# A two-layer hybrid decoder trunk on one core: every read of SBUF by GpSimd in the mixing stages goes to ScalarE and VectorE

## The chip, the core and the metric

The kernel runs on one core of a Trainium2 chip. The core's engines each work through their own instruction queue in order and meet at semaphores: TensorE (PE in the profile, with its weight loads as PEld), VectorE (DVE), ScalarE (ACT), GpSimd (POOL) and SyncE (SP), which issues the DMAs. The metric is the device time of one execution in microseconds. The kernel before takes 1375.88 us (median of three runs, 1375.21 to 1383.43).

## What is computed

Two decoder layers over 512 tokens of width 1024, in float32. The reference, cut:

```python
for l in range(DEPTH):                                   # DEPTH = 2
    h = rmsnorm(x, g_mix[l])
    (cq, ckv, kr, aq, ak, av, qi, ki, wi, rq, rk, rv, rg) = split(h @ w_in[l])
    # A) latent attention, 8 heads: low-rank q (768) and kv (256), rotary part of 32
    q  = rmsnorm(cq, g_q[l]) @ w_uq[l];  kv = rmsnorm(ckv, g_kv[l]) @ w_ukv[l]
    o_a = mla_attention(q_nope, rope(q_rope), k_nope, rope(kr), v)
    # B) sparse attention, 4 heads: an indexer scores all keys, the best 128 of a query are kept
    score = einsum(wi, relu(rope(qi) . rope(ki)));  sel = top_k(score, 128)
    o_b = dsa_attention(rope(aq), rope(ak), av, sel)
    # C) retention, 4 heads, with group norm and swish gate
    o_c = silu(rg) * groupnorm(retention(rope(rq), rope(rk), rv))
    x = x + concat(o_a, o_b, o_c) @ w_out[l]
    hf = rmsnorm(x, g_mlp[l])
    x = x + square(relu(hf @ w_ff1[l])) @ w_ff2[l]
return rmsnorm(x, g_final)
```

## The kernel before, in words

Activations are held transposed: a tile has 128 features on the partitions and the 512 tokens in its columns. To keep float32 precision, each operand of a matmul is split into a high half (rounded to the type fp32r) and a low half (the rest), and a product is three matmuls: high by high, high by low, low by high (`mm3`). So nearly every tile costs one copy for the high half and one subtraction for the low half, for weights (`wsplit`, `wh` and `wl`) as for activations (`split`), and for the exponentials of attention (`exp_split`: `pe` is the exponential, `hi` and `lo` its halves, written side by side in a `p` tile).

A layer has a mixing stage (layer 1: from the start to about 345 us; layer 2: about 685 to 1027 us) and an MLP stage. The MLP stage sets `mode` to `hi="a"`, `lo="v"`: ScalarE makes its high halves and VectorE its low halves, and GpSimd has nothing to do. In the mixing stage the engine of each piece is chosen by short strings at the head of the file, one letter for each piece in turn ('a' ScalarE, 'v' VectorE, 'p' GpSimd): `MHI` and `MLO` for the weights' halves (`H0` for the first two), `E_ROT` for the two products of a rotary embedding with its table (`rope`), `E_SS` for sums of squares (`sumsq_add`), `E_MSK` for the causal mask of a retention score (`ret_score`), `SPA` and `SPD` for the exponentials of the latent and the sparse attention. In `exp_split` the letter 'p' means: exponential on ScalarE, high half copied on GpSimd, low half on VectorE; 'b' means exponential and copy on ScalarE, low half on VectorE; 'e' means a second exponential on ScalarE straight into the high half, and the low half on GpSimd. In `ret_done` (group norm and gate of two retention heads) four operations are written for GpSimd by name.

The order of the work is written out by hand: `ORDER` names steps of the mixing stage (`qi0`, `cq3`, `a0` for a half of a pair of attention heads, `d2` for a query block of sparse attention), with `tN` for N top-k operations and `rN` for N retention scores as fillers. A top-k round (`top_round`, L748 and L749) takes eight maxima of a row of index scores and strikes them out; 16 rounds for each of three query blocks, then a mask (L753). `PRI` shifts groups of instructions in the scheduler's priorities (-225 for top-k, that is later; 99 for weights, earlier). The scheduler lays out each engine's queue from these and from its own estimate of durations. `LAG` lets the product with V run four score tiles behind the scores; scores have three PSUM banks (`sc`), exponentials three buffers (`pe`) and six for their halves (`p`).

Of the kernel before, what the change touches and what calls it, by code (L numbers as in the profile page):

```python
# [13 lines left out]
AF = mybir.ActivationFunctionType  # L14
ALU = mybir.AluOpType
# [16 lines left out]
OPT_O = 2  # L32
WARM = 14
E_ADD = 'v'
SPA = 'pb'
SPD = 'ppe'
RD = 'dd'
NFULL = 6
NPE1 = 3
NPE2 = 7  # L40
NEMIT = 4
H0 = 'ap'
L0 = 'v'
W2K = 2
SQ = 'aavaavaa'
OPT_X = 0
OPT_T = 0
E_SS = 'p'
E_ROT = 'pv'
E_RCP = "v"  # L50
E_MSK = 'p'
OPT_D = 1
OPT_S = 0
OPT_R = 0
MHI = 'aaap'
MLO = 'vp'
ORDER = 'qi0 rg0 qi1 tk ix1 ix2 F rq0 ix3 rk0 rq1 r1 t2 r1 r1 t3 rk1 t4 rg1 aq1 r1 r1 aq0 F t2 t2 F F F F F t2 F F kv0 kv1 F F t1 F F r2 cq0 t2 t2 r1 r1 cq1 r4 kvf kvc t2 cq2 cq3 t5 r7 cq4 t1 t4 r16 t4 t2 cq5 r12 F F r6 r12 t1 F r2 v0 r16 r14 F r14 r9 cqf r2 t4 mk F t2 r1 r2 cqc r2 r2 r3 F t1 r11 rr0 t1 t4 t4 q0 r4 k1 t5 F k0 t2 r4 F t2 r2 q1 t4 r6 t4 r2 F t10 t10 t3 t4 m0 r2 r6 t2 r5 m1 r3 r2 r1 t3 t2 t5 a0 a1 t2 k2 t4 t4 dm t7 t4 r10 r1 t9 rr1 r1 t7 t3 r2 t4 a2 q2 a3 q3 t3 r3 m2 r7 t6 r10 r2 d2 t5 d3 d0 t15 d1 k3 t4 t2 r2 t2 t1 t3 m3 v1 a4 t8 t1 a6 F t3 r2 t4 t59 t2 r1 t6 r2 a7 r2 t3 t1 t3 a5 t2 t3 F r1 F r3 r2 r10 F r2 F'
PRI = {'fin': 0, 'w': 99, 'e': 59, 't': -225, 'rope': 0, 'split': 133, 'q': -16, 'qm': 0, 'rr': 0, 'v': 5, 'k': 0, 'att': 0, 'pv': 0, 'done': -70, 'ret': -44, 'st': 65, 'x': 0, 'tab': -20, 'cq': 0, 'tok': 15, 'idx': 0, 'dm': 8, 'rg': 0, 'km': 0, 'qi': 0, 'aq': 0}
TOPK = 128
# [12 lines left out]
def trunk_kernel(ctx, tc, xT, gains, win, wtk, wuq, wukv, wout, wff1, wff2, tabs, cf, cb, outT):  # L72
    nc = tc.nc
# [6 lines left out]

    count = {"n": 0, "w": 0, SPA: 0, SPD: 0}

    def hp(k):
        return tc.high_priority(PRI[k]) if PRI[k] else nullcontext()
# [8 lines left out]
    def g_(dt=F32, shape=None):  # L93
        return S("g", GB, shape, dt)
# [15 lines left out]
    def u2():  # L110
        return pair("u", 8)
# [16 lines left out]
    def sc_ps():  # L128
        return pp.tile([P, T], F32, tag="sc", bufs=3, name=nm("sc"))
# [4 lines left out]
    def R(ap):  # L134
        return ap.bitcast(F32)

    def tt(eng, op, out, a, b):
        (nc.vector if eng == "v" else nc.gpsimd).tensor_tensor(out, a, b, op=op)  # L138

    def mm(out, lhsT, rhs, start, stop):  # L140
        return nc.tensor.matmul(out, lhsT, rhs, start=start, stop=stop)  # L141
# [38 lines left out]
    def gcol(i):  # L180
        return gn[:, i : i + 1]
# [3 lines left out]
    def copy_fr(out, src, eng):  # L185
        if eng == "a":
            return nc.scalar.activation(out, src, AF.Copy)  # L187
        if eng == "p":
            return nc.gpsimd.tensor_scalar(out, src, 1.0, 1.0, op0=ALU.mult, op1=ALU.mult)  # L189
        return nc.vector.tensor_copy(out, src)  # L190
# [7 lines left out]
    def wsplit(raw, width, parts):  # L198
        res = []
        w = width // parts  # L200
        for c in range(parts):
# [3 lines left out]
            count["w"] += 1  # L205
            ins = copy_fr(hi, rc, H0[n] if n < len(H0) else mode["hi"][n % len(mode["hi"])])
            if ins.ins.engine == order["uh"].ins.engine:
# [23 lines left out]
    def split(src, hi, lo, eng="a"):  # L231
        copy_fr(hi, src, eng)
        nc.vector.tensor_sub(lo, src, R(hi))  # L233
# [35 lines left out]
    def sumsq_add(ss, src, first, last=False):  # L269
        if first:  # L270
            nc.scalar.activation(ss, src, AF.Square)
        else:
            s = g_()
            nc.scalar.activation(s, src, AF.Square)
            tt("v" if OPT_S and last else E_SS, ALU.add, ss, ss, s)

# [21 lines left out]
    def rope(zz, tab, swaps):  # L298
        with hp("rope"):
            z, zs = zz[:, 0], zz[:, 1]  # L300
            ct, st = tab
            for dst, src in swaps:
                nc.sync.dma_start(zs[dst], z[src])
            tt(E_ROT[0], ALU.mult, z, z, ct)
            tt(E_ROT[1], ALU.mult, zs, zs, st)
            tt(E_ADD, ALU.add, z, z, zs)
# [14 lines left out]
    def push(f):  # L321
        pend.append(f)
        while len(pend) > LAG:
            pend.popleft()()
# [284 lines left out]
    for l in range(DEPTH):  # L609
        G0 = l * G_LAYER  # L610
        mode.update(hi=MHI, lo=MLO)
        begun, ready = {}, {}
# [182 lines left out]
        def ret_score(pr, e, i):  # L795
# [12 lines left out]
            mb = m01[:, 2 * P - w :].rearrange("p (o n) -> p o n", o=1).to_broadcast([P, 2, w])  # L808
            tt(E_MSK, ALU.mult, pt[:, :, :w], R(pt[:, :, :w]), mb)
            v = vt[2][:, i, 2 * pr + e]  # L810
            push(lambda: pv_step("r", i, [(v, ph), (v, pl)], lambda o: ret_done(pr, e, o)))

        def ret_done(pr, e, o):
            with hp("ret"):
                rows = slice(64 * e, 64 * e + 64)
                if e == 0:
                    rts[pr] = g_()
                rt = rts[pr]
                half = g_()
                nc.scalar.activation(half[rows], o[64 - 64 * e : 128 - 64 * e], AF.Copy)  # L820
                nc.vector.tensor_add(rt[rows], o[rows], half[rows])
                if e == 0:
                    return
                sg = sgs[pr]
                sq = g_()
                nc.scalar.activation(sq, rt, AF.Square)
                ps = sc_ps()
                mm(ps, blk, sq, True, True)
                yv = g_()
                nc.scalar.activation(yv, ps, AF.Ln, bias=epst)  # L830
                nc.scalar.activation(yv, yv, AF.Exp, scale=-0.5)
                nc.gpsimd.tensor_mul(sq, yv, yv)
                nc.vector.scalar_tensor_tensor(sq, ps, EPS, sq, op0=ALU.add, op1=ALU.mult)
                nc.gpsimd.tensor_scalar(sq, sq, -0.5, 1.5, op0=ALU.mult, op1=ALU.add)
                nc.gpsimd.tensor_mul(yv, yv, sq)
                nc.vector.scalar_tensor_tensor(rt, rt, gcol(G0 + G_RET + pr), yv, op0=ALU.mult, op1=ALU.mult)
                nc.gpsimd.tensor_mul(rt, rt, sg)
                mh, ml = u2()
                split(rt, mh, ml)
                mix[6 + pr] = (mh, ml)  # L840
# [101 lines left out]
        vv = {}  # L942
# [122 lines left out]
        def pair_attn(gp, heads=(0, 1)):  # L1065
            rd, pr = divmod(gp, 2)
            vh, vl = vv[rd]
            for e in heads:
# [4 lines left out]
                for i in range(NB):  # L1073
# [12 lines left out]
                    ph, pl = pt[:, 0], pt[:, 1]  # L1086
                    exp_split(ps, A_SCALE, ph, pl, SPA)
                    terms = [(vh[:, i, pr, cs], ph), (vh[:, i, pr, cs], pl), (vl[:, i, pr, cs], ph)]
                    push(lambda i=i, terms=terms, e=e: pv_step("a", i, terms, lambda o: pair_done(gp, e, o)))

        def exp_split(ps, scale, hi, lo, pattern):
            how = pattern[count[pattern] % len(pattern)]
            count[pattern] += 1
            pe = S("pe", PEB)[:, : ps.shape[1]]
            if how == "e":
                nc.scalar.activation(hi, ps, AF.Exp, scale=scale)
            nc.scalar.activation(pe, ps, AF.Exp, scale=scale)  # L1097
            if how != "e":
                copy_fr(hi, pe, "p" if how == "p" else "a")
            tt("p" if how in "ea" else "v", ALU.subtract, lo, pe, R(hi))  # L1100
# [26 lines left out]
        def dsa_pv(j, i, ph, pl):  # L1127
            with hp("pv"):
                if i == 0:
                    dsa_o[0] = o_ps()  # L1130
                o = dsa_o[0]
                mm3(o, vt[0][:, i, 0:128], vt[1][:, i, 0:128], ph, pl, i == 0, i == j)
                if i < j:
                    return
                js = slice(j * P, (j + 1) * P)
                hs = slice(64, 128)
                s, y, oh = g_(), g_(), g_()
                nc.scalar.activation(s[hs], o[0:64], AF.Copy)
                if OPT_D:
                    nc.scalar.activation(oh[hs], o[hs], AF.Copy)  # L1140
                recip(y[hs], s[hs])
                nc.vector.tensor_mul(y[hs], (oh if OPT_D else o)[hs], y[hs])
                nc.vector.scalar_tensor_tensor(s[hs], s[hs], 2.0, y[hs], op0=ALU.subtract, op1=ALU.mult)
                oh = oh.bitcast(FR)
                nc.scalar.activation(oh[hs], s[hs], AF.Copy, scale=-1.0)
                s4 = s[hs].rearrange("p (t e n) -> p t e n", t=2, e=2)
                h4 = oh[hs].rearrange("p (t e n) -> p t e n", t=2, e=2)
                for h in range(4):
                    rows = slice(64 * (h % 2), 64 * (h % 2) + 64)
                    nc.scalar.activation(mix[4 + h // 2][0][rows, js], s4[:, h // 2, h % 2], AF.Copy, scale=-1.0)  # L1150
                    nc.vector.scalar_tensor_tensor(mix[4 + h // 2][1][rows, js], s4[:, h // 2, h % 2], -1.0,
                                                   R(h4[:, h // 2, h % 2]), op0=ALU.mult, op1=ALU.subtract)

        def dsa_score(j, i):
# [9 lines left out]
            ph, pl = pp_[:, 0], pp_[:, 1]  # L1164
            exp_split(ps, B_SCALE, ph, pl, SPD)
            push(lambda: dsa_pv(j, i, ph, pl))
# [199 lines left out]
```

## Time and profile before

| | |
|---|---|
| median of three runs | 1375.88 us |
| the profiled execution | 1376.64 us |
| its span, first to last instruction | 1374.9 us |
| PE busy in the span | 1317.4 us (96%) |
| DVE busy | 1091.4 us (79%) |
| ACT busy | 670.6 us (49%) |
| POOL busy | 323.3 us (24%) |
| mean granted clock of PE, as a share of full speed | 0.979 |

Busy times are averages over stages with different limits, so the rows below cut the span into stretches. "Idle before" in a row is the time that the engine stood still before these instructions. A mean duration in nanoseconds belongs to one instruction; neighbours on VectorE and ScalarE overlap a little, so a sum of durations is somewhat above the busy time.

### The profile page before, as it was taken

The page shows a single profiled execution, that of the slowest core. Times are in us where ns is not written, and L with a number is a line of the kernel's source. Part 1 is how long each engine was busy: PE and PEld are TensorE (multiplying, and loading weights), DVE is VectorE, ACT ScalarE, POOL GpSimd, SP SyncE. Part 2 cuts the span into 40 slices and gives each one's busy share as a digit, 9 for nine tenths or more (in the row PEclk, how much of TensorE's full clock was granted, in tenths as well). Part 3 has the DMA queues.
Part 4 walks back from the last instruction along what each step waited for, and adds up shares of the span by engine and source line. Part 5 has one row for each costly group of instructions (what it writes and reads, how often), then busy time and mean ns, then how long its engine had stood idle before and what let it go on. Part 6 is the DMA issues. An engine that isn't in the chain of part 4 may idle for free.

```text
span 1374.9 us, 20315 instructions
## 1 busy us (share of the span) xinstructions
PE 1317.4 (96%) x7358; PEld 1112.0 (81%) x7360; DVE 1091.4 (79%) x1846; ACT 670.6 (49%) x1189; POOL 323.3 (24%) x325
## 2 busy tenths in 40 slices
PE   9989989899999999999999999898999999999997
PEld 7867766677888888899997767666778888889997
DVE  5799998977777767787769999868757877777875
ACT  4534545784444444555535345447744444445552
POOL 3456743425000000000043566333330000000000
PEclk9999999999999999999999999889999999999998
DMA  6568222203455554475545652221135554554662
GB/s 217 158 188 213 71 88 86 78 16 112 164 169 183 174 180 154 157 241 185 197 132 173 171 151 67 80 78 39 46 108 169 186 183 167 157 194 157 205 185 69
DMA packets 75779, 197.55 MB, mean 144 GB/s; under 512 B 8960, under 2 KB 13792, under 8 KB 75680
## 3 DMA queue, kind: packets, MB, share of 16 engines
q1 hardware_dynamic: 74528, 195.22, 46.0%
q8 instruction: 58, 0.95, 0.3%
q10 hardware_dynamic: 1152, 1.05, 0.2%
q14 instruction: 41, 0.34, 0.1%
HBM read 155.68 MB, written 20.97 MB: 128 GB/s over the span
## 4 chain that ended last, share of the span: by engine, by line
PE 71%; DVE 16%; ACT 4%; issue 4%; DMA 3%; POOL 1%; POOLq 0%; SPq 0%; DVEq 0%; ACTq 0%
PE mm L141 40%; PE sc L503 11%; PE sc L141 5%; PE mm L503 5%; PE o L503 5%; PE o L141 3%; DVE p L138 2%; DVE g L749 2%; DVE wl L210 2%; DVE m L748 1%; DMA wr<-in_win 1%; DVE g L741 1%; DMA wr<-in_wff 1%; DVE g L233 1%; PE sc L363 1%
## 5 line engine op out<-in xcount | busy, mean ns | idle before, releaser
L141 PE MATMUL mm<-u,wh 128*128 128x512 f32 (+1 forms) x1776 | 552.0, 390 | 0.0
L141 PEld LDWEIGHTS mm<-u,wh 128*128 128x128 f32 x1776 | 331.3, 190 | 65.2 <-issue 0.8
L141 PE MATMUL mm<-u,wl 128*128 128x512 f32 (+1 forms) x888 | 345.6, 389 | 0.7 <-DVE wl L210 0.7
L187 ACT ACTIVATE wh<-wr 128x512 fp32r<-128x512 f32 (+2 forms) x247 | 149.9, 610 | 294.6 <-PE mm L141 183.0
L210 DVE TENSOR_TENSOR wl<-wr,wh 128x512 fp32r<-128x512 f32 (+2 forms) x208 | 154.4, 743 | 85.3 <-ACT wh L187 82.0
L212 POOL TENSOR_TENSOR wl<-wr,wh 128x512 fp32r<-128x512 f32 (+2 forms) x80 | 105.4, 1318 | 434.6 <-ACT wh L187 413.8
L141 PEld LDWEIGHTS mm<-u,wl 128*128 128x128 f32 x888 | 168.3, 190 | 35.6 <-DVE wl L210 1.1
L141 PE MATMUL o<-p,v 128*128 128x512 f32 (+2 forms) x316 | 82.7, 369 | 6.0 <-DVE p L138 2.7
L490 DVE TENSOR_TENSOR u<-wr,u 128x1024 fp32r<-128x1024 f32 x54 | 66.0, 1222 | 26.0 <-ACT u L489 25.8
L489 ACT ACTIVATE u<-wr 128x1024 fp32r<-128x1024 f32 x54 | 57.2, 1059 | 54.3 <-PE mm L503 16.0
L432 DVE TENSOR_TENSOR sm<-wr 128x512 f32<-128x512 f32 x64 | 44.4, 694 | 46.9 <-DMA wr<-in_wff 46.9
L503 PEld LDWEIGHTS sc<-g,v 128*128 128x128 f32 x576 | 72.2, 189 | 2.3
L503 PE MATMUL sc<-g,v 128*128 128x256 f32 x576 | 73.1, 281 | 0.0
L141 PEld LDWEIGHTS o<-p,v 128*128 128x128 f32 x316 | 52.5, 198 | 15.8 <-DVE p L138 5.7
L189 POOL TENSOR_SCALAR p<-pe 128x512 fp32r<-128x512 f32 (+1 forms) x46 | 38.9, 850 | 74.2 <-ACT pe L1097 71.0
L138 DVE TENSOR_TENSOR p<-pe,p 128x256 fp32r<-128x256 f32 (+2 forms) x78 | 48.6, 648 | 9.4 <-POOL p L189 7.0
L420 DVE SCALAR_TENSOR_TENSOR g<-mm,g 128x512 f32<-128x512 f32 x64 | 43.9, 686 | 14.4 <-PE mm L141 14.3
L749 DVE MATCH_REPLACE8 g<-m,g 128x512 f32<-128x512 f32 (+2 forms) x96 | 51.3, 537 | 0.0
L503 PE MATMUL o<-g,v 128*128 128x256 f32 x384 | 50.5, 281 | 0.0
L436 ACT ACTIVATE v<-wr 128x1024 fp32r<-128x1024 f32 x32 | 34.0, 1064 | 33.4 <-DVE wr L434 33.4
L141 PE MATMUL sc<-u,qk 97*128 97x512 f32 (+5 forms) x192 | 47.4, 357 | 2.8 <-ACT pe L1097 2.7
L748 DVE MAX8 m<-g 128x8 f32<-128x256 f32 (+2 forms) x96 | 49.8, 544 | 0.1
(301 smaller groups left out, 2718.2 us busy)
## 6 DMA issues: line engine op xcount, KB each, us to landing
wr<-in_wff SPq DMA_DIRECT2D x160, 512.0 KB, 3.9
wr<-in_win SPq DMA_DIRECT2D x37, 512.0 KB, 7.1
ws<-sm SPq DMA_DIRECT2D x32, 512.0 KB, 5.8
wr<-ws SPq DMA_DIRECT2D x32, 512.0 KB, 4.5
tab<-in_tabs SPq DMA_DIRECT2D x20, 512.0 KB, 5.0
wr<-in_wout SPq DMA_DIRECT2D x16, 512.0 KB, 3.6
p<-p SPq DMA_DIRECT2D x40, 128.0 KB, 2.2
wr<-in_wuq SPq DMA_DIRECT2D x12, 384.0 KB, 3.5
```

Of the source, the lines that this page charges most:

```text
L138: (nc.vector if eng == "v" else nc.gpsimd).tensor_tensor(out, a, b, op=op)
L141: return nc.tensor.matmul(out, lhsT, rhs, start=start, stop=stop)
L187: return nc.scalar.activation(out, src, AF.Copy)
L210: order["wl"] = nc.vector.tensor_sub(lo, rc, R(hi))
L212: nc.gpsimd.tensor_sub(lo, rc, R(hi))
L420: nc.vector.scalar_tensor_tensor(r, ps, 0.0, rb, op0=ALU.max, op1=ALU.mult)
L432: nc.vector.tensor_add(sm[:, h], w[0], w[1])
L489: nc.scalar.activation(wh, t, AF.Copy)
L490: nc.vector.tensor_sub(wl, t, R(wh))
L503: nc.tensor.matmul(outs[m][0], a[:, m * P : m * P + P], b, start=i == 0 and outs[m][1] and n == 0, stop=i == KP - 1 and n == 2, skip_group ...
L748: nc.vector.max(m8, accs[j])
L749: nc.vector.match_replace(out=accs[j], in_to_replace=m8, in_values=accs[j], imm_value=GONE)
```

## The change

In the mixing stages GpSimd reads nothing from SBUF any more. ScalarE makes all high halves: of weights (`H0`, `MHI`) and of exponentials (`SPA`, `SPD` at 'b', so there is no second exponential either). VectorE makes all low halves (`MLO`, and those of the former 'e' tiles), both table products of the rotary embeddings (`E_ROT`), the masks (`E_MSK`) and the sums of squares (`E_SS`). In `ret_done` the square and the scaling go to ScalarE and the two products to VectorE. GpSimd keeps its memsets, which only write. `ORDER`, `PRI`, the buffers and the MLP stage stay as they are.

```diff
 E_ADD = 'v'
-SPA = 'pb'
-SPD = 'ppe'
+SPA = 'b'
+SPD = 'b'
 RD = 'dd'
...
-H0 = 'ap'
+H0 = 'aa'
 L0 = 'v'
...
-E_SS = 'p'
-E_ROT = 'pv'
+E_SS = 'v'
+E_ROT = 'vv'
 E_RCP = "v"
-E_MSK = 'p'
+E_MSK = 'v'
...
-MHI = 'aaap'
-MLO = 'vp'
+MHI = 'a'
+MLO = 'v'
...
                 nc.scalar.activation(yv, yv, AF.Exp, scale=-0.5)
-                nc.gpsimd.tensor_mul(sq, yv, yv)
+                nc.scalar.activation(sq, yv, AF.Square)
                 nc.vector.scalar_tensor_tensor(sq, ps, EPS, sq, op0=ALU.add, op1=ALU.mult)
-                nc.gpsimd.tensor_scalar(sq, sq, -0.5, 1.5, op0=ALU.mult, op1=ALU.add)
-                nc.gpsimd.tensor_mul(yv, yv, sq)
+                nc.scalar.activation(sq, sq, AF.Copy, scale=-0.5, bias=1.5)
+                nc.vector.tensor_mul(yv, yv, sq)
                 nc.vector.scalar_tensor_tensor(rt, rt, gcol(G0 + G_RET + pr), yv, op0=ALU.mult, op1=ALU.mult)
-                nc.gpsimd.tensor_mul(rt, rt, sg)
+                nc.vector.tensor_mul(rt, rt, sg)
```

## Rows read from the trace of the kernel before

**Rows 1.** The page, part 1: busy us, share of the span, instructions.
```profile
PE 1317.4 (96%) x7358; PEld 1112.0 (81%) x7360; DVE 1091.4 (79%) x1846; ACT 670.6 (49%) x1189; POOL 323.3 (24%) x325
```
**Rows 2.** The page, part 2: GpSimd's busy tenths in 40 equal slices.
```profile
POOL 3456743425000000000043566333330000000000
```
**Rows 3.** Stretches: length; busy us (instructions) by engine; granted clock; DMA share, GB/s.
```profile
70.00:210.00 140.00, 128.88 (x561) 98.60 (x561) 135.98 (x278) 59.93 (x115) 80.35 (x78) 0.96 0.49 136
735.00:875.00 140.00, 128.20 (x538) 99.15 (x538) 133.28 (x272) 60.05 (x114) 81.17 (x80) 0.93 0.49 138
210.00:245.00 35.00, 34.29 (x173) 23.67 (x174) 28.62 (x54) 20.31 (x43) 14.23 (x16) 1.00 0.36 117
875.00:910.00 35.00, 35.00 (x154) 22.72 (x153) 23.77 (x43) 10.81 (x24) 8.64 (x9) 0.85 0.16 44
245.00:306.00 61.00, 53.76 (x304) 41.39 (x302) 53.31 (x85) 49.73 (x104) 21.90 (x25) 0.97 0.09 30
910.00:987.00 77.00, 66.65 (x365) 50.17 (x364) 65.55 (x103) 60.15 (x126) 27.79 (x35) 0.98 0.18 56
```
**Rows 4.** The page, part 4: the chain of waits by engine.
```profile
PE 71%; DVE 16%; ACT 4%; issue 4%; DMA 3%; POOL 1%; POOLq 0%; SPq 0%; DVEq 0%; ACTq 0%
```
**Rows 5.** Groups on POOL, 70 to 210: busy us, mean ns | idle before.
```profile
L212 POOL TENSOR_TENSOR wl<-wr,wh 128x512 fp32r<-128x512 f32 x11 | 16.4, 1491 | 10.2 <-PE mm L141 5.8 <-PE sc L141 2.7 <-ACT wh L187 1.4
L138 POOL TENSOR_TENSOR p<-p,cft 128x256 fp32r<-128x256 f32 x12 | 9.9, 834 | 7.0 <-DVE p L233 4.4 <-PE mm L141 1.8 <-DVE tiny L238 0.7
L138 POOL TENSOR_TENSOR p<-p,tab 128x512 f32<-128x512 f32 x6 | 9.5, 1587 | 5.0 <-DVE g L741 3.4 <-DMA p<-p 0.8 <-DMA tab<-in_tabs 0.8
L138 POOL TENSOR_TENSOR ss<-ss,g 128x512 f32<-128x512 f32 x6 | 7.8, 1295 | 3.4 <-ACT ss L271 1.9 <-ACT g L274 1.4
L212 POOL TENSOR_TENSOR wl<-wr,wh 128x384 fp32r<-128x384 f32 x6 | 6.4, 1068 | 5.8 <-ACT wh L187 5.7
L138 POOL TENSOR_TENSOR p<-p,cft 128x512 fp32r<-128x512 f32 x4 | 6.2, 1540 | 0.0
```
**Rows 6.** Groups on DVE in the MLP stage, 350 to 665.
```profile
L210 DVE TENSOR_TENSOR wl<-wr,wh 128x512 fp32r<-128x512 f32 x58 | 39.8, 687 | 30.4 <-ACT wh L187 29.3 <-PE mm L141 1.2
L420 DVE SCALAR_TENSOR_TENSOR g<-mm,g 128x512 f32<-128x512 f32 x31 | 21.2, 685 | 5.4 <-PE mm L141 5.4
L449 DVE TENSOR_TENSOR g<-g,g 128x256 fp32r<-128x256 f32 x16 | 6.7, 416 | 0.0
```
**Rows 7.** Groups on DVE, 70 to 210.
```profile
L210 DVE TENSOR_TENSOR wl<-wr,wh 128x512 fp32r<-128x512 f32 x13 | 10.2, 788 | 0.0
L748 DVE MAX8 m<-g 128x8 f32<-128x512 f32 x15 | 10.1, 676 | 0.0
...
L741 DVE SCALAR_TENSOR_TENSOR g<-g,wtok,g 128x512 f32<-128x512 f32 x7 | 7.0, 1005 | 0.0
...
L210 DVE TENSOR_TENSOR wl<-wr,wh 128x384 fp32r<-128x384 f32 x6 | 6.1, 1017 | 1.1 <-ACT wh L187 1.1
L233 DVE TENSOR_TENSOR g<-p,g 128x512 fp32r<-128x512 f32 x5 | 5.6, 1118 | 0.0
```
**Rows 8.** Timelines of DVE and PE: start us, us, instruction.
```profile
222.91 0.35 DVE L753 TENSOR_SCALAR ma<-g 128x384 bf16<-128x384 f32 x1
...
225.99 0.50 PE L141 MATMUL sc<-ma,cbt 128*128 128x384 bf16 x2
```
**Rows 9.** Groups on POOL, 245 to 306 (first two) and 910 to 987.
```profile
L189 POOL TENSOR_SCALAR p<-pe 128x512 fp32r<-128x512 f32 x11 | 8.7, 798 | 23.5 <-ACT pe L1097 23.5
...
L189 POOL TENSOR_SCALAR p<-pe 128x256 fp32r<-128x256 f32 x4 | 3.3, 824 | 3.3 <-ACT pe L1097 2.5 <-PE sc L141 0.8
...
L189 POOL TENSOR_SCALAR p<-pe 128x512 fp32r<-128x512 f32 x13 | 10.8, 838 | 23.3 <-ACT pe L1097 23.3
```
**Rows 10.** ACT: timeline from 196 us; group in 245 to 306.
```profile
196.36 2.59 ACT L187 ACTIVATE u<-g 64x512 fp32r<-64x512 f32 x4 [1.13 <-DVE g L991]
...
L187 ACT ACTIVATE p<-pe 128x256 fp32r<-128x256 f32 x4 | 1.7, 414 | 0.1
```

## The prediction

> **What bounds the kernel now.** I read the busy shares first. TensorE (PE) is busy for 96% of the span and VectorE (DVE) for 79%; GpSimd (POOL) has 24% [rows 1]. The slices then show where GpSimd works: in slices 1 to 10 and 21 to 30, the two mixing stages, and nowhere else [rows 2]. All that the change can win or lose lies there.
>
> The table by stretch says what is lost in them [rows 3]. In 70 to 210 us (layer 1: index scores, top-k, low-rank query, retention scores) PE is busy for 128.9 of 140 us, while DVE is busy for 136.0: DVE is the fuller engine. Layer 2's counterpart, 735 to 875, has 128.2 and 133.3. In the attention stretches, 245 to 306 and 910 to 987, PE has 53.8 of 61 and 66.7 of 77, DVE 53.3 and 65.6, ScalarE (ACT) 49.7 and 60.2. PE's idle time over the six stretches is 11.1 + 11.8 + 0.7 + 0 + 7.2 + 10.4 = 41 us. A clock share c below 1 over t us is (1 - c)t of lost work: 0.04 x 140 + 0.07 x 140 + 0.15 x 35 + 0.03 x 61 + 0.02 x 77 = 24 us. So 65 us is about all that better feeding could give. The chain of waits puts 16% of the span on DVE, 4% on ACT and 1% on POOL [rows 4]: the engine that gives work away is nearly never the one waited for, and the one that receives most of it often is.
>
> **The change part by part.** Every POOL operation that reads SBUF goes; memsets stay, and no DMA is moved, so SP's queue is as before.
>
> *To DVE in the top-k stretch.* In 70 to 210 the POOL groups that move to DVE are 11 weight low halves, 6 rotary products, 6 sums of squares and 4 masks of 512 columns (27), 6 low halves of 384 and 12 masks of 256 [rows 5]; a few smaller groups are left out. DVE's price without POOL beside it is that of the MLP stage: 0.687 us for 512 columns, 0.416 for 256 [rows 6]; for 384 I put 0.55 between them. The sum is 27 x 0.687 + 6 x 0.55 + 12 x 0.416 = 18.5 + 3.3 + 5.0 = 26.8 us of DVE.
>
> *What DVE gets back there.* DVE operations that read two SBUF tiles run long in this stretch: L210 at 0.788 (512) and 1.017 (384), L741 at 1.005, L233 at 1.118, against 0.687 or, for the L741 kind, 0.685 in the MLP stage [rows 6, 7]. The excess is 13 x 0.101 + 6 x 0.467 + 7 x 0.32 + 5 x 0.431 = 1.3 + 2.8 + 2.2 + 2.2 = 8.5 us. Many small groups are alike; I take twice that, 16 us, as an estimate, with 8.5 and the whole 26.8 as bounds. MAX8, which reads one tile, stays at 0.676 and gets nothing back [rows 7]. The Trainium skill, "SBUF — State Buffer", section "Who interferes with whom", has the same line of division: a VectorE instruction with two SBUF inputs contends with a GpSimd instruction that reads SBUF, one with a single input does not. The trace agrees. By that rule it speaks against this change in a top-k stretch, where GpSimd's help is free, and for it elsewhere.
>
> The net is 26.8 - 16 = +11 us (bounds 0 and +18) on a DVE that has 4.0 us idle in layer 1 and 6.7 in layer 2 [rows 3]: an overrun of 7 and 4 us. The top-k rounds can slide, since DVE has 6.4 and 11.2 us idle in the next 35 us [rows 3], until PE needs the masks: layer 1's last mask is written by 223.3 and its matmul starts at 225.99, 2.7 us of slack [rows 8]. Queued behind a late round on DVE are the low halves of weights and queries, and PE waits for these. I take 7 - 2.7, about +4, for layer 1 and half of 4, +2, for layer 2: **+6 us**, bounds 0 and, with +18 net, 14 + 11 = +25.
>
> *To ACT in attention.* In 245 to 306 POOL makes 11 high halves of exponentials with 512 columns and 4 with 256; layer 2 has 13 of the wide ones [rows 9], and I count 4 narrow ones there too. ACT's copies go at 2.59 / 4 = 0.65 us for 512 columns and 0.414 for 256 [rows 10]. That adds 11 x 0.65 + 4 x 0.414 = 8.8 us to 49.7 of 61, and 13 x 0.65 + 4 x 0.414 = 10.1 us to 60.2 of 77: at the old length ACT goes from 82% to 96% and from 78% to 91%. The exponential frees the score bank for PE, and each new copy stands between two exponentials on ACT, so the next score matmul waits for it. The fullest in-order engine in this trace is DVE at 97% (136 of 140), so the stretches could keep their length; at 85% they would be 58.5 / 0.85 = 68.8 and 70.3 / 0.85 = 82.7 us, +7.8 and +5.7. I take 90%: 65.0 and 78.1, **+5 us** together, bounds 0 and +13. DVE is no bound here: it has 53.3 of 61 and is relieved of POOL beside it.
>
> *Shorter links.* A POOL operation on the chain becomes a DVE or ACT one: 1.491 to 0.687, or 0.798 to 0.65 [rows 5, 6, 9, 10]. POOL's 1% of the chain is 13.7 us (rounding: 6.9 to 20.6) [rows 4]; half of it goes, **-7 us**, bounds -3 and -10. The group-norm operations of L832 to L837 and the sums of squares that close the output projection are links of this kind.
>
> The sum is +6 + 5 - 7 = +4 us on the profiled execution's 1376.64 us (span 1374.9 and 1.7 around it; the median of the runs is 1375.88): **1381 us**. The bounds together give -10 to +35.
>
> **The rivals.**
> 1. *The relief wins (faster).* DVE operations shorten everywhere, products of rotary tables, scores and residues arrive sooner, PE's gaps close and the clock stays up. For it: L233 at 1.118 and L741 at 1.005, both on chains that PE waits for. Against: the full engine gets as much as it is rid of. If 40% of the 65 us came back, 1376.6 - 26 = 1350. The Trainium skill, "GPSIMD Engine Reference", section "4.1 Engine selection", advises this outcome: elementwise work on VectorE, GpSimd being about 2x slower with two inputs; the trace has 1.491 against 0.687.
> 2. *DVE's queue binds (slower).* The top-k rounds do not slide: DVE takes the whole +18 net in each layer, masks come late, and the score maxima of the sparse heads hold PE. It decides once the last mask is written after its matmul's old place (226 us in layer 1). Price 14 + 11 = +25: 1402.
> 3. *Nothing shows.* ACT and DVE both find room, PE's order hides it all: 1376 give or take 5. For it: ACT is busy for only 20.3 and 10.8 us of the 35 us before the attention stretches [rows 3].
>
> **How the numbers follow.** About 1% (13.8 us) is what a measurement of this kernel can tell from no change, so "faster" ends at 1362 and "slower" begins at 1390. My forecast has 0.45, with a range of its own of 1366 to 1398: 0.33 of it within 1%, 0.12 beyond. Rival 1 has 0.20, all faster; rival 2 0.22, all slower; rival 3 0.13, within. That is faster 0.20, same 0.46, slower 0.34. The engine orders are laid out anew by the scheduler, which no row prices; it widens every case. The range 1360 to 1408 leaves out the longer half of rival 1 (0.12) and the tail of rival 2 (0.08).
>
> **What would show it.** Right: POOL down to memsets; two-tile DVE operations at 0.69 throughout; DVE at 97% or more in the top-k stretches with MAX8 ending later than before; ACT above 90% in the attention stretches with PE waiting for L1097 or a copy at L187; the mixing stages a few us longer and the MLP stages unchanged. Wrong: if the top-k stretches end no later although DVE has more to do (the excess was bigger than 16 us), if ACT's share in attention stays near 80%, or if PE's clock in the mixing slices rises to full, which is rival 1.

## The result, and the profile after

The changed kernel takes 1392.51 us (median of four runs, 1390.36 to 1396.05) against 1375.55 us for the kernel before in the same comparison: a ratio of 1.0104, interval 1.0066 to 1.0142. Its profiled execution took 1390.69 us with a span of 1388.9, 14.0 more than the span before.

The page after, part 1 (busy us, share, instructions), one line of part 2 (TensorE's granted clock in 40 slices, tenths) and the chain of waits by engine:

```profile
PE 1324.7 (95%) x7360; PEld 1114.4 (80%) x7360; DVE 1099.0 (79%) x2020; ACT 716.0 (52%) x1284; POOL 25.6 (2%) x56
...
PEclk9999997899999999999999998969999999999999
...
PE 86%; DVE 8%; ACT 4%; issue 2%; DMA 1%; DVEq 0%
```

GpSimd is down from 323.3 us to 25.6, all memsets. VectorE has 174 more instructions than in [rows 1] and only 7.6 us more busy time: nearly all that it took over it got back in shorter operations. Its share of the chain halves from 16% to 8% [rows 4]. By these three numbers alone one would expect a gain. The clock line shows two dips: slices 7 and 8 (about 208 to 278 us), and slices 25 and 27 (833 to 868 and 903 to 938 us).

The same stretches as [rows 3], then the two attention stretches moved to where attention lies now, then two pieces of the first dip (length; busy us by engine PE, PEld, DVE, ACT, POOL; granted clock; DMA share, GB/s):

```profile
70.00:210.00 140.00, 130.96 (x584) 101.22 (x583) 130.59 (x283) 70.24 (x136) 8.56 (x14) 0.98 0.48 129
735.00:875.00 140.00, 130.94 (x568) 102.08 (x567) 131.42 (x298) 75.79 (x155) 8.55 (x14) 0.96 0.54 142
210.00:245.00 35.00, 25.60 (x87) 14.67 (x85) 31.94 (x80) 11.16 (x22) 1.96 (x4) 0.77 0.30 98
875.00:910.00 35.00, 32.23 (x154) 23.41 (x153) 32.31 (x75) 14.58 (x32) 0.98 (x2) 0.91 0.17 47
261.00:322.00 61.00, 54.70 (x301) 41.88 (x300) 46.95 (x87) 56.01 (x120) 0.29 (x2) 0.97 0.06 18
928.00:1005.00 77.00, 69.81 (x376) 52.99 (x375) 59.74 (x110) 66.44 (x142) 1.06 (x4) 0.93 0.11 35
222.00:233.00 11.00, 6.07 (x19) 4.60 (x20) 11.00 (x31) 3.04 (x5) 0.98 (x2) 0.82 0.66 216
233.00:253.00 20.00, 17.53 (x44) 8.68 (x44) 15.97 (x32) 4.97 (x11) 0.00 (x0) 0.50 0.31 104
```

Up to 210 us everything is better than before: PE busier, its clock higher, VectorE less full. In 210 to 245 PE does 87 matmuls where it did 173. From 222 to 233 VectorE has no idle time at all while PE stands for 4.9 of 11 us, and in the 20 us after that PE runs at a granted clock of 0.50, the level of 1.2 GHz, while it counts as busy for 17.53.

What PE waited for, over the whole run (us, times, longest):

```profile
PE sc L141 <- DVE ma L753: 12.7, 4, 5.6
PE mm L141 <- DVE v L965: 11.1, 4, 3.8
...
PE mm L141 <- DVE g L991: 5.8, 2, 2.9
...
PE sc L141 <- ACT pe L1097: 3.0, 8, 0.6
```

The first line is new; before, PE never waited for L753, the top-k masks. PE's and VectorE's timelines at that place in layer 1 (start us, us, instruction, idle before and its releaser):

```profile
227.45 0.62 PE L141 MATMUL mm<-g,wh 128*128 128x512 f32 x2
233.64 0.37 PE L141 MATMUL sc<-ma,cbt 128*128 128x256 bf16 x1 [5.57 <-DVE ma L753]
...
232.51 0.41 DVE L749 MATCH_REPLACE8 g<-m,g 128x256 f32<-128x256 f32 x1
232.84 0.56 DVE L748 MAX8 m<-g 128x8 f32<-128x384 f32 x1
233.30 0.28 DVE L753 TENSOR_SCALAR ma<-g 128x256 bf16<-128x256 f32 x1
...
237.73 0.69 DVE L753 TENSOR_SCALAR ma<-g 128x384 bf16<-128x384 f32 x2
```

The score maxima of the sparse heads (L1115) need a mask as a matmul operand (`sc<-ma`). From 222 to 233.30 VectorE has no gap: it is at top-k rounds and, between them, at rotary products and low halves. PE's next matmul needs the mask, and PE stands. The last mask comes after 237.7; in [rows 8] it started at 222.91.

First starts of some lines, and the gain or loss that they divide the run into (us):

| | before | after | after - before |
|---|---|---|---|
| layer 1: group norm, L833 | 148.9 | 140.8 | -8.1 |
| top-k masks, L753, first and last | 210.4, 222.9 | 233.3, 238.0 | +22.9, +15.1 |
| MLP, L420 | 348.6 | 362.1 | +13.5 |
| layer 2: token weights, L713 | 720.5 | 734.7 | +14.2 |
| group norm, L833 | 820.9 | 823.0 | +2.1 |
| top-k masks, L753, first and last | 863.5, 884.1 | 916.3, 921.0 | +52.8, +36.9 |
| MLP, L420 | 1030.0 | 1045.0 | +15.0 |
| span | 1374.9 | 1388.9 | +14.0 |

Each layer first gains and then loses: -8.1 and +21.6 in layer 1, -12.1 and +12.9 in layer 2, with the MLP stages unchanged within 1 us. So nearly the whole net loss is layer 1's, between its group norm and its MLP stage, where the masks lie.

### The profile page after: what moved, and what is told of

Same layout as the page of the kernel before. It is cut to its first block, busy times and chain, and to the rows that moved or that the text cites. A ratio compares the mean times of both kernels' runs of the same rounds, so it can differ in the third digit from the quotient of the medians.

```text
span 1388.9 us, 20133 instructions
## 1 busy us (share of the span) xinstructions
PE 1324.7 (95%) x7360; PEld 1114.4 (80%) x7360; DVE 1099.0 (79%) x2020; ACT 716.0 (52%) x1284; POOL 25.6 (2%) x56
## 4 chain that ended last, share of the span: by engine, by line
PE 86%; DVE 8%; ACT 4%; issue 2%; DMA 1%; DVEq 0%
PE mm L141 51%; PE sc L503 11%; PE sc L141 8%; PE mm L503 5%; PE o L503 5%; PE o L141 4%; DVE g L749 2%; DVE m L748 1%; DVE p L138 1%; ACT pe L1097 1%; ACT p L187 1%; DMA wr<-in_wff 1%; DVE wl L210 1%; PE sc L629 0%; PE sc L363 0%
## 5 line engine op out<-in xcount | busy, mean ns | idle before, releaser
L187 ACT ACTIVATE wh<-wr 128x512 fp32r<-128x512 f32 (+3 forms) x288 | 173.5, 607 | 344.7 <-PE mm L141 243.4
L210 DVE TENSOR_TENSOR wl<-wr,wh 128x512 fp32r<-128x512 f32 (+3 forms) x288 | 188.6, 658 | 103.2 <-ACT wh L187 98.9
L138 DVE TENSOR_TENSOR p<-pe,p 128x512 fp32r<-128x512 f32 (+1 forms) x84 | 45.3, 562 | 19.8 <-ACT p L187 18.7
L141 PE MATMUL mm<-x,wh 128*128 128x512 f32 x96 | 38.9, 485 | 18.3 <-DVE v L965 7.4
L420 DVE SCALAR_TENSOR_TENSOR g<-mm,g 128x512 f32<-128x512 f32 x64 | 43.9, 687 | 13.2 <-PE mm L141 12.9
L141 PE MATMUL sc<-u,qk 97*128 97x512 f32 (+5 forms) x192 | 52.8, 389 | 1.4 <-ACT pe L1097 1.2
L749 DVE MATCH_REPLACE8 g<-m,g 128x384 f32<-128x384 f32 (+2 forms) x96 | 51.5, 543 | 0.0
L748 DVE MAX8 m<-g 128x8 f32<-128x256 f32 (+2 forms) x96 | 50.3, 550 | 0.1
L503 PEld LDWEIGHTS o<-g,v 128*128 128x128 f32 x384 | 47.5, 189 | 0.0
```

Source lines behind the costliest of these rows:

```text
L210: order["wl"] = nc.vector.tensor_sub(lo, rc, R(hi))
L420: nc.vector.scalar_tensor_tensor(r, ps, 0.0, rb, op0=ALU.max, op1=ALU.mult)
L503: nc.tensor.matmul(outs[m][0], a[:, m * P : m * P + P], b, start=i == 0 and outs[m][1] and n == 0, stop=i == KP - 1 and n == 2, skip_group ...
L748: nc.vector.max(m8, accs[j])
L749: nc.vector.match_replace(out=accs[j], in_to_replace=m8, in_values=accs[j], imm_value=GONE)
```

## The experiments

Theory L (load): GpSimd's share of the work cost nothing beside the top-k rounds; on VectorE it delays them, and PE pays at the masks. Theory A: ScalarE, fuller in attention, delays the exponentials (the prediction's second term). Theory M (meeting): VectorE has room, and only the new order puts a mask just ahead of the matmul that needs it. In the recorded expectations up to the runs that move the maxima, "Theory M" means late masks from either cause, load or order; from there on L is split off from it as the "Load theory". Ratios are to the kernel before, run beside each experiment, with their intervals; its median was between 1375.55 and 1383.02 us from one comparison to the next, so ratios are compared here and not times. Edits are to the kernel named.

**Half of the top-k rounds, in the changed kernel and in the one before.** Both kernels leave out rounds 9 to 16 of each query block, so their masks keep 64 keys in place of 128.

```diff
-        for _ in range(TOPK // 8):
+        for _ in range(TOPK // 16):
```

> The kernel after with half of the top-k rounds left out (8 of 16, so fewer keys are struck out). Theory M (late masks: the top-k rounds stand too late in VectorE's queue, the sparse heads' masks come 15 to 23 us later than before and TensorE stands still for them, then runs at a lower clock): some 25 us of VectorE a layer go, the waits of sc<-ma for L753 vanish, and the time falls by 30 us or more from 1392, to 1362 or less, and below the run with half the rounds of the kernel before. Theory A (ScalarE's added copies in attention are the loss): the loss stays beside e2, so about 10 to 16 us above it.

> The kernel before with the same half of the top-k rounds left out. Theory M: there the masks were in time, so the gain is smaller, 5 to 15 us (1360 to 1370), and e1 ends up 5 to 20 us below it because VectorE is no longer slowed by GpSimd. Theory A: 10 to 16 us below e1.

The changed kernel falls to 1355.16 us, 0.9788 (0.9729 to 0.9847); the one before to 1368.91, 0.9895 (0.9837 to 0.9953). Half of the rounds is about 50 us of VectorE's work: on the page after, L748 and L749 take 50.3 and 51.5 us for both layers. Taking it off gives 0.0316 x 1376 = 43 us in the changed kernel and 14 us in the one before, and of the two the changed kernel is now the faster by 14 us. The stretch that was lost, in the changed kernel with half of the rounds (columns as above):

```profile
210.00:245.00 35.00, 35.00 (x190) 24.66 (x190) 28.36 (x49) 21.59 (x46) 2.05 (x6) 1.00 0.31 99
```

No idle time, no fall of the clock, no wait for L753. The loss hangs on the top-k rounds, as L says (M needs them too), and what remains is the relief. A is out of favour already: attention was not touched.

**The exponentials back on GpSimd** (changed kernel).

```diff
-SPA = 'b'
-SPD = 'b'
+SPA = 'pb'
+SPD = 'ppe'
```

> The kernel after with the exponentials' halves as before (SPA 'pb', SPD 'ppe'): 46 high halves back on GpSimd, 6 exponentials straight into the high half. Theory A: the loss was ScalarE in attention, so 1372 to 1380. Theory M: the masks are as late as in the kernel after, so 1385 to 1396.

1394.78 us, 1.0099 (1.0062 to 1.0136): nothing comes back. The attention stretches and the wait for the masks in this kernel:

```profile
261.00:322.00 61.00, 56.51 (x323) 42.33 (x323) 51.37 (x90) 53.61 (x112) 17.39 (x23) 1.00 0.06 19
928.00:1005.00 77.00, 72.75 (x368) 53.21 (x368) 63.39 (x108) 58.33 (x121) 18.51 (x26) 0.88 0.09 28
...
PE sc L141 <- DVE ma L753: 22.1, 4, 10.3
```

ScalarE goes from 66.4 to 58.3 of 77 us in the second, and the time does not follow. The longer wait for the masks (22.1 us in place of 12.7) does not hide a gain: from the last mask to the MLP stage it is 123.2 and 123.7 us in the two layers, 124.1 and 124.0 in the changed kernel. Theory A falls.

**Top-k rounds earlier**, in the changed kernel and in the one before.

```diff
-PRI = {..., 't': -225, ...}
+PRI = {..., 't': -130, ...}
```

> The kernel after with one number changed: the top-k rounds' priority -130 instead of -225, so that VectorE's queue has all three masks ahead of the first score maximum of the sparse heads, as the kernel before nearly had. Same instructions on the same engines. Theory M: the waits for L753 go and the relief of the first half of the mixing stage remains: 1350 to 1372, below the kernel before. Theory A: no change beyond 5 us, 1387 to 1397.

> The kernel before with the top-k rounds' priority at -130 in place of -225: the same engines, only the queue order of e4. In the kernel before the masks were in time, so Theory M sees nothing to win: 1374 to 1390. If the order alone moves the time as much as the whole change does, this is under 1368 or over 1390, and a difference of 10 us between e4 and the kernel after says little.

The changed kernel gains some: 1385.97 us, 1.0026 (0.9999 to 1.0054). The kernel before gains nothing: 1382.65, 0.9993 (0.9961 to 1.0025). In the changed kernel the wait for L753 is gone and another stands in its place, with a dip of the clock that now lies at 194 to 215 us:

```profile
PE sc L141 <- DVE tiny L1025: 12.5, 2, 6.6
...
194.00:215.00 21.00, 13.44 (x43) 8.95 (x44) 19.53 (x45) 2.78 (x5) 0.00 (x0) 0.51 0.12 39
```

The maxima of the latent attention (L1025) are now queued behind the rounds. The time lies between the two ranges that were expected. So about 0.8% of the time hangs on the order in which the changed kernel happens to be laid out, and that is against L as far as it goes; but in this order too PE waits, and the change does not win in it (1.0026 to 0.9993, with intervals that overlap).

**The causal masks of the retention scores back on GpSimd** (changed kernel; L138, `p<-p,cft`, not the top-k masks).

```diff
-E_MSK = 'v'
+E_MSK = 'p'
```

> The kernel after with the retention masks (E_MSK) back on GpSimd: 12 operations of 256 and 4 of 512 columns a layer, some 7.7 us of VectorE in the top-k stretch, while the rest of the change stays. Theory M with VectorE's capacity in the top-k stretch as the cause: masks of the sparse heads some 5 us earlier a layer than in the kernel after, and 1376 to 1388. If only the place of the top-k rounds in the queue matters and not VectorE's load: 1389 to 1396, as the mask still stands behind the first score maxima in the queue.

1380.71 us, 1.0002 (0.9971 to 1.0034). These are 32 products, 24 of 256 columns and 8 of 512, on VectorE 24 x 0.419 + 8 x 0.683 = 15.5 us. Rid of them the kernel gains 0.0102 x 1376 = 14 us, near one for one. The top-k masks start at 227.8 and PE still waits 13.3 us for them, so the gain is not that this wait got shorter. It lies ahead of the masks: from the group norm to the first mask it is 85.1 and 87.0 us in the two layers, 92.5 and 93.3 in the changed kernel; from the last mask to the MLP stage it is 124.2 and 124.4, as in the changed kernel.

**Parts of the change alone, on the kernel before**: the weights' halves; and the rotary products, sums of squares and the group-norm operations.

```diff
-H0 = 'ap'
+H0 = 'aa'
...
-MHI = 'aaap'
-MLO = 'vp'
+MHI = 'a'
+MLO = 'v'
```

> The kernel before with the weights' halves alone moved (H0, MHI to ScalarE, MLO to VectorE). VectorE gets about 12 us a layer more in the top-k stretch (11 low halves of 512, 6 of 384), GpSimd keeps rotary products, sums, masks and copies. Theory M: this is the largest part of the load, so most of the loss: 1382 to 1395, with the wait for L753. If the loss is spread evenly over the parts: about a third of it, 1378 to 1384.

```diff
-E_SS = 'p'
-E_ROT = 'pv'
+E_SS = 'v'
+E_ROT = 'vv'
...
-                nc.gpsimd.tensor_mul(rt, rt, sg)
+                nc.vector.tensor_mul(rt, rt, sg)
```

> The kernel before with the rotary products, the sums of squares and the group norm alone moved. These stand in chains that TensorE waits for in the first half of the mixing stage, and bring VectorE some 11 us a layer in the top-k stretch. Theory M: the first half gains 4 to 8 us a layer, the masks come later and take most of it back: 1372 to 1386. If contention with GpSimd's weight halves is what slows VectorE, little gain in the first half: 1380 to 1392.

1376.83 us, 0.9983 (0.9958 to 1.0008), and 1376.26 us, 0.9957 (0.9926 to 0.9988): neither loses, though the first was expected to under both theories, and the second gains a little. Yet both already show the wait for L753 that the kernel before has not:

```profile
PE sc L141 <- DVE ma L753: 9.9, 4, 4.4
...
PE sc L141 <- DVE ma L753: 9.2, 4, 3.9
```

So about 10 us of that wait can stand beside a kernel that is no slower. The parts do not add up: -0.2% and -0.4% alone, and 0.0% (1.0002) with both moved and the exponentials besides. It is the third part on top, the retention masks, that tips the sum: with them on VectorE and only the exponentials on GpSimd 1.0099, with them on GpSimd 1.0002. Those alone on the kernel before were not tried.

**The sparse heads' maxima later** (`dm` moved behind `a3` in `ORDER`): in the changed kernel, in the changed kernel with the retention masks on GpSimd, and in the one before.

```diff
-ORDER = '... t2 k2 t4 t4 dm t7 t4 ... a2 q2 a3 q3 ...'
+ORDER = '... t2 k2 t4 t4 t7 t4 ... a2 q2 a3 dm q3 ...'
```

> The kernel after with the step dm (the sparse heads' score maxima, which read the masks) put behind two more halves of attention in ORDER (after a3); VectorE's queue up to the masks stays as it was, the matmuls that read a mask come some 40 places later in TensorE's queue. Theory M: TensorE works through attention while the masks are made, the wait for L753 (6.3 us a layer) and the low clock behind it go, so 1366 to 1380. If VectorE's load itself is the loss, and not the order in which TensorE meets it: another wait takes its place and it stays at 1386 to 1396.

> e9 with the retention masks on GpSimd as in e5 (VectorE some 7.7 us a layer freer in the top-k stretch). Theory M: below e9 by 5 to 12 us and below the kernel before: 1358 to 1372. Load theory: about e5, 1376 to 1384.

> The kernel before with the same move of dm in ORDER, to see what the move is worth by itself. There the masks were in time, so Theory M: no gain, 1372 to 1386. If the move is good whatever the engines do, it gains as much here as in e9 against the kernel after.

1393.17 us, 1.0117 (1.0076 to 1.0159); 1379.03, 1.0020 (0.9983 to 1.0056); 1373.76, 0.9972 (0.9940 to 1.0004). In the first the meeting of mask and matmul is gone and nothing is won. Its waits, PE and VectorE at the longest of them, and the stretch at half clock:

```profile
PE o L141 <- DVE p L138: 8.1, 4, 3.3
...
233.89 1.22 PE L141 MATMUL o<-p,v 128*128 128x384 f32 x3 [3.30 <-DVE p L138]
...
233.29 0.54 DVE L138 TENSOR_TENSOR p<-pe,p 128x384 fp32r<-128x384 f32 x1
...
233.00:271.00 38.00, 34.26 (x106) 21.04 (x108) 29.73 (x60) 13.77 (x27) 1.07 (x4) 0.51 0.18 64
```

Theory M falls: without the meeting PE waits for low halves of exponentials (`p<-pe,p`), which stand between the same top-k rounds in VectorE's queue, and the clock is down for longer. The second run repeats the gain of 1% that the retention masks gave in the other order.

**Help from GpSimd only where the top-k rounds run** (changed kernel): the retention masks, and in the two steps that lie in the stretch (`kv`, `cq`) every second low half of a weight tile and the sums of squares.

```diff
-E_MSK = 'v'
+E_MSK = 'p'
...
-            tt("v" if OPT_S and last else E_SS, ALU.add, ss, ss, s)
+            tt(mode.get("ss", E_SS), ALU.add, ss, ss, s)
...
             n = int(num or 0)
+            help_ = name in ("kv", "cq")
+            mode.update(lo="vp" if help_ else MLO, ss="p" if help_ else E_SS)
```

> The kernel after, with GpSimd reading SBUF again only where VectorE is full of top-k rounds: the retention masks, and in the steps kv and cq every second low half of the weights and the sums of squares. Everything else stays on VectorE and ScalarE. Load theory (VectorE's net load in the top-k stretch is the loss, its relief in the rest of the mixing stage the gain; e9 has shown that the order alone only moves the wait): below e5 and below the kernel before, 1362 to 1374. Theory M (only the meeting of the mask and its matmul counts): no better than e5, 1377 to 1386, as the mask still stands behind the first score maxima in the queue.

1366.51 us (1363.34 to 1370.30), 0.9911 (0.9887 to 0.9934): faster than the kernel before, and with that than the changed one. What GpSimd does in it beside memsets, and the top-k stretches:

```profile
L212 POOL TENSOR_TENSOR wl<-wr,wh 128x512 fp32r<-128x512 f32 x16 | 22.6, 1412 | 43.3 <-ACT wh L187 37.8 <-PE sc L141 2.7 <-DMA wr<-in_win 2.6
L138 POOL TENSOR_TENSOR p<-p,cft 128x256 fp32r<-128x256 f32 x24 | 20.7, 877 | 33.0 <-DVE p L233 30.8 <-DVE tiny L238 1.4 <-DVE tiny L237 0.7
L138 POOL TENSOR_TENSOR ss<-ss,g 128x512 f32<-128x512 f32 x12 | 18.6, 1552 | 9.9 <-ACT g L274 6.1 <-ACT ss L271 3.7
L138 POOL TENSOR_TENSOR p<-p,cft 128x512 fp32r<-128x512 f32 x8 | 11.1, 1392 | 0.0
...
70.00:210.00 140.00, 136.23 (x624) 105.06 (x623) 132.63 (x286) 75.15 (x148) 47.11 (x46) 0.99 0.48 132
735.00:875.00 140.00, 134.48 (x620) 103.43 (x618) 132.71 (x284) 75.44 (x149) 44.83 (x46) 1.00 0.47 130
```

GpSimd works for 73 us at these groups, where the kernel before has some 298 (the 323.3 us of [rows 1] less 25.6 of memsets). PE is busy for 136.2 and 134.5 us, against 128.9 and 128.2 in [rows 3]. The group norm of layer 2 starts at 811.3 us, 9.6 before its place in the kernel before, and the MLP stage at 1018.4, 11.6 before it; layer 1 comes out even (347.9 to 348.6). PE still waits 10.6 us for L753, so this version too has not got rid of the wait.

## Why the prediction was right, and where it was not

**The load on VectorE (first term): right in its way, too small in its price.** Between the last index score and the last top-k mask VectorE has to do all rounds and what lies beside them. The stretch between these two, layer 1 and layer 2, before, then after, then layer 1 with GpSimd's help (columns as above):

```profile
86.50:223.30 136.80, 127.94 (x571) 96.67 (x569) 131.40 (x282) 60.00 (x118) 75.10 (x73) 0.96 0.44 120
753.00:884.50 131.50, 122.29 (x538) 93.80 (x536) 126.21 (x269) 54.12 (x104) 75.47 (x73) 0.95 0.45 121
...
80.40:238.40 158.00, 139.83 (x613) 105.36 (x612) 147.65 (x337) 74.47 (x144) 7.60 (x12) 0.95 0.44 120
762.00:921.40 159.40, 141.22 (x614) 106.46 (x614) 148.27 (x338) 74.35 (x144) 7.59 (x12) 0.93 0.43 118
...
79.50:224.50 145.00, 136.34 (x616) 103.11 (x615) 137.17 (x307) 74.25 (x144) 47.02 (x44) 0.96 0.47 131
```

VectorE's busy time in it grows by 16.3 us in layer 1 and 22.1 in layer 2, and the stretch by 21.2 and 27.9. Not all of that is load that was moved. Counted group by group (operations times mean duration), 27.6 us moved over in layer 1 and 29.0 in layer 2, near the 26.8 of the sum; what VectorE had to do there already got shorter by 12.7 and 14.2 us, where I took 16; so the net is about +15 in both, between my +11 and its bound of +18. Another 6.0 and 12.4 us is work that the new layout put into the stretch, and VectorE stands idle in it for 5.0 and 5.8 us more than before. (Neighbours overlap, so durations add up to more than busy time.) Many of VectorE's operations there are MAX8 and MATCH_REPLACE8, which have nothing to get back. MATCH_REPLACE8 in the whole run, before and after:

```profile
L749 DVE MATCH_REPLACE8 g<-m,g 128x512 f32<-128x512 f32 (+2 forms) x96 | 51.3, 537 | 0.0
...
L749 DVE MATCH_REPLACE8 g<-m,g 128x384 f32<-128x384 f32 (+2 forms) x96 | 51.5, 543 | 0.0
```

The groups of [rows 7] in 70 to 210 after the change:

```profile
L210 DVE TENSOR_TENSOR wl<-wr,wh 128x512 fp32r<-128x512 f32 x25 | 17.1, 689 | 2.9 <-ACT wh L187 2.7
L748 DVE MAX8 m<-g 128x8 f32<-128x512 f32 x11 | 7.5, 684 | 0.0
L210 DVE TENSOR_TENSOR wl<-wr,wh 128x384 fp32r<-128x384 f32 x11 | 6.1, 550 | 0.4 <-ACT wh L187 0.4
L741 DVE SCALAR_TENSOR_TENSOR g<-g,wtok,g 128x512 f32<-128x512 f32 x7 | 5.2, 750 | 0.0
L233 DVE TENSOR_TENSOR g<-p,g 128x512 fp32r<-128x512 f32 x5 | 3.4, 683 | 0.0
```

The two-tile operations go to 0.689 and 0.550 as foretold, L741 from 1.005 to 0.750, L233 from 1.118 to 0.683, and MAX8 stays (0.676 to 0.684). Only 11 of its wide ones lie in the window, 15 before: the scheduler laid the rounds later. That is why VectorE is at 93% (130.6 of 140) in 70 to 210 and not at the 97% that I named as a sign; it is full in 222 to 233 instead. The sign was right and its place wrong.

**The place was rival 2's.** The last mask was written after 226 us (238), the point from which that rival decides. The slack of 2.7 us was used up and PE waited 6.3 us a layer. But the price is not the wait: with the exponentials back on GpSimd the wait is 22.1 us in all and not 12.7, at the same ratio. What decides is when the last mask comes. From its start to the start of the MLP stage (us):

| | layer 1 | layer 2 |
|---|---|---|
| before | 125.7 | 145.9 |
| after | 124.1 | 124.0 |
| after, exponentials back on GpSimd | 123.2 | 123.7 |
| after, retention masks back on GpSimd | 124.2 | 124.4 |
| after, help beside the top-k rounds | 123.8 | 124.4 |

In the changed kernel and these three versions of it the figure hardly moves (in the two parts alone and in the changed kernels of the other orders it is 123 to 130), so there the last mask seems to set the end of the mixing stage. The kernel before takes 1.6 us more in layer 1 and 21.9 more in layer 2: by so much its last mask could have come later. Of the 15.1 us that it comes later, layer 1 pays 13.5; of 36.9, layer 2 pays 15.0. In layer 1 one can follow where PE loses them: it is idle for 7.7 us in 215 to 233 (10.28 busy of 18); then, in 20 us at a clock of 0.50, it is busy for 17.53, half of which (8.8) is lost, and idle for 2.5: together 19 of the 21.6 us that the table of starts has for this half of the layer.

The step that failed is "7 - 2.7, about +4, for layer 1". Its net load of +11 measures +15; the overrun of 7 that it gave became a stretch 21.2 us longer, since other work and idle time came into it as well; and no term stood for the clock that PE loses with it. The slack was near right (2.7, and 1.6 by the table). The clock is 1.00 in that stretch of [rows 3]; the 0.85 of layer 2's counterpart, 875 to 910, was the hint that it can fall there.

**ScalarE in attention (second term): wrong.** Its share rose to 92% (56.0 of 61) and 86% (66.4 of 77), a little less than computed, although layer 2 has 6 narrow copies and not the 4 that I counted. But PE's waits for L1097 are 3.0 us in all (3.7 before), and the exponentials' copies back on GpSimd gave 1.0099 for 1.0104. The +5 is about nothing. The error was to take a full engine for a late one, with no wait in the rows that said so; what hid the copies (the score banks, or the product with V running four tiles behind) no run separates.

**Shorter links (third term): right in sign, too small.** POOL is off the chain and VectorE's share halves. The first halves of the layers gain 8.1 + 12.1 = 20 us where the term had 7. How much of it is shorter links and how much the relief of single operations, no run separates. L741, the index scores, shows how uneven it is (layer 1, before and after; ns min/median/max, first and last start):

```profile
L741 DVE SCALAR_TENSOR_TENSOR g<-g,wtok,g x21: 473/607/1772, 59.0 to 86.5; 128x256 f32<-128x256 f32 x7, 128x384 f32<-128x384 f32 x7, 128x512 f32<-128x512 f32 x7
...
L741 DVE SCALAR_TENSOR_TENSOR g<-g,wtok,g x21: 479/614/753, 56.9 to 80.4; 128x256 f32<-128x256 f32 x7, 128x384 f32<-128x384 f32 x7, 128x512 f32<-128x512 f32 x7
```

The medians are alike and the longest falls from 1.772 to 0.753 us: here contention struck few operations and those hard, and a mean over a group hides what a link on the chain loses.

**The sum.** +6 and +5 and -7 stood for +34 (21.6 + 12.9), 0 and -20. Two large terms of opposite sign made a small net. That 1381 came within 12 us of 1392.5 is luck in the signs: no term had its size right. The result lies inside the forecast's own range, 1366 to 1398, and just beyond the bound of 1%; the interval reaches to both sides of that bound. Rival 1 was right about the relief and wrong that it would be kept; rival 2 had the place, with +25 for a loss of 34 and no relief set against it; rival 3 falls.

**The rule of the port.** Of the groups above the two-tile ones got shorter when GpSimd stopped reading, and MAX8 did not. The Trainium skill, "SBUF — State Buffer", section "Who interferes with whom", divides VectorE's instructions in the same way, by two SBUF inputs or at most one (outside VectorE's 2-port modes); the trace agrees. The prediction held the consequence in one sentence (GpSimd's help is free in a top-k stretch, dear elsewhere), and the last experiment is that sentence made into a kernel. The Trainium skill, "GPSIMD Engine Reference", section "4.1 Engine selection", advises doing elementwise work on VectorE. Followed in the whole of the mixing stages this gave 1.0104, and 0.9911 when left aside beside the top-k rounds alone; there the measurement decides against it.

**What stays open.** Why the clock falls, and why it stays at 0.50 for 20 us and longer after the wait; whether an order made anew by hand would remove the last version's 10.6 us of waits, or make the full change win; and how much of each ratio is load and how much the scheduler's new layout, which every edit brings with it. Earlier rounds alone gave the changed kernel 0.8%, less load beside them 1.0%.

## What to carry to other kernels

Before work is moved off a slow helper engine, sort what the receiving engine does at that time into operations that the helper disturbs and operations that it does not; beside the second kind the slow helper was nearly free here. Find the first thing behind that stretch that another engine needs from it, and price how much later it will come than its room allows: the wait that a profile shows is not that price, and TensorE can lose clock besides. A high share of an engine is no cost until a row shows somebody waiting for it.

## What the runs showed of the hardware that I had not expected

The low clock outlasts the wait by far. In the changed kernel PE was busy for 10.28 of the 18 us ahead of it; then it ran at 0.50 from 233 to 253 us, busy for 17.53 of 20 with 44 matmuls, and at 1.00 in the 10 us after, with 70:

```profile
215.00:233.00 18.00, 10.28 (x37) 7.25 (x37) 17.70 (x48) 5.00 (x9) 0.98 (x2) 0.89 0.40 132
...
253.00:263.00 10.00, 10.00 (x70) 8.18 (x69) 8.20 (x15) 8.52 (x17) 1.06 (x4) 1.00 0.19 57
```

With the maxima moved later it stayed down for 38 us (0.51) with PE busy for 34.26 of them. A busy share near 90% there is a slow PE, not a well-fed one: the granted clock has to be read beside it. Nor does a low clock need a wait ahead of it. In layer 2 of the kernel before PE counted as busy without a break from 884 us on, yet while it worked through the sparse heads' maxima it ran at 0.50:

```profile
884.00:888.00 4.00, 4.00 (x28) 3.29 (x27) 3.49 (x8) 3.87 (x11) 2.58 (x3) 1.00 0.27 109
...
896.00:900.00 4.00, 4.00 (x12) 2.36 (x10) 2.27 (x4) 0.00 (x0) 0.00 (x0) 0.50 0.00 0
```
